# Two heads on the row halves of TensorE in a chunked gated linear attention

## Chip, cores and metric

The kernel runs on one core of one Trainium2 chip. The metric is the device time in microseconds of one execution. A core has five engines that the text names by the profile's short names: PE (TensorE: matmuls; PEld are its weight loads), DVE (VectorE), ACT (ScalarE), POOL (GpSimd) and SP (SyncE, which issues DMAs). Matmuls write into PSUM, which has 128 partitions and eight banks of 512 float32 per partition; the other operands lie in SBUF, also on 128 partitions. A matmul takes a stationary operand (rows by columns, loaded as weights) and a moving operand, and sums over the rows, which are the partitions of both. In the profile, `128*32 128x224` is a matmul of weights with 128 rows and 32 columns against 224 moving columns. A float32 matmul shows as two such records.

## The reference, cut to what matters

One layer of a streaming encoder: a normalised and modulated input is projected, two recurrences (GLA and HGRN2) of four heads each run over it, and their gated outputs are projected back. The prompt has 4096 positions, the sample 64. The recurrence is the same for both; GLA has 64 key features per head and HGRN2 has 128, both 128 value features:

```python
'''S_t = diag(exp g_t) S_{t-1} + k_t^T v_t,  o_t = q_t S_t.'''
def step(S, inp):                       # one chunk
    qc, kc, vc, gc = inp
    b = jnp.cumsum(gc, axis=2)
    o_inter = jnp.einsum('bhck,bhkv->bhcv', qc * jnp.exp(b), S)
    ...                                 # within the chunk: decayed q k^T, causal, times v
    S_new = (S * jnp.exp(b_last)[..., None]
             + jnp.einsum('bhck,bhcv->bhkv', kc * jnp.exp(b_last[:, :, None] - b), vc))
    return S_new, o_inter + o_intra.reshape(B, H, CHUNK, V)
```

All inputs and outputs are float32.

## The kernel before

The prompt is cut into 16 groups of 256 positions (two chunks of 128). First the GLA projections and recurrence run for all groups, then those of HGRN2, then the output projection. The sample's 64 positions lie beside the last GLA group and beside an early HGRN2 group.

`proj_gla` projects a group: queries and keys by feature (`proj_feat`, L559), the silu gate and the low-rank decay gate (`z_part`, L571 with 264 columns), values (L571 with 512 columns). These matmuls use float32 split into two parts, three products each. `x_turn` transposes the next group's input (L506) into the one bank `tp`, from which ACT (L515) and DVE (L517) take it.

`attend` is the recurrence over a group, as a generator that stops 14 times in GLA. Features lie on the partitions. GLA's heads have 64 features, so two heads share the 128 partitions: `NS` is 2, `G` (feature blocks per chunk) is 2 and `VG` (both chunks) is 4. HGRN2 has `NS` 1, `G` 4 and `VG` 8. The scores within a chunk are built by levels, blocks of positions that double:

- Positions 1, 2 and 4 apart: products by feature, turned by PE (L635) and summed by DVE (L641).
- `three_levels` does levels 2 to 4 at once. `prepare` fills a tile `wst` with queries decayed by distance (DVE L836, ACT L848, POOL memsets L846 and L843), PE multiplies them with blocks of 32 keys (L878) into a bank `at`, DVE picks the valid parts into `Ac` (`copy_predicated`, L892), ACT spreads these into the scores `A` (L898), and `times` (L836 on `Qg` and `K`) brings queries and keys to the next level.
- Levels 5 and 6, in a loop: matmuls into a bank `at` (L718), `step` on queries and keys (DVE L804 and L807), ACT copies into `A` (L728).
- Per chunk: keys by token (L740), outputs from the scores (L752) and from the state (L756) into the bank `o`, the state's increment (L764) into the bank `ms`, the new state (DVE L775), the gate's product (`done`, DVE L1082) and the squares for the norm (ACT L783), which read the bank `o`.

The array sums over all 128 rows, so in GLA the queries `Qg` are stored twice, once for each head of the pair, with the other head's 64 rows zero: ACT copies them there (L680). All work on `Qg` is then done per half, with DVE instructions on 64 partitions.

PSUM has three banks `pj` (projections), one `tp`, two `at`, one `o` and one `ms`, eight in all. A bank is handed on when all its readers are through.

The order of the work comes from `weave`: the projections of group g + 1 are the main generator (20 stops in GLA), and between its stops run the stops of `attend` of group g and of `x_turn`:

```python
sides = [(side, 12, 1, 18), (prep, 8, 0, 16)]
...
while s[4] * (last - first) < n * (m - first):
    s[4] += 1
    next(gen, None)
```

With 12 and 1 to 18, the steps 7 to 13 of `attend` come after the main stops 10, 11, 13, 14, 16, 17 and 19 (steps counted from the second stop of the generator on). A compiler pass then lays out each engine's queue; it keeps to this order by and large, and puts a later instruction first where it expects an earlier one to wait.

Of the kernel before, what the change touches and what calls it, by code (L numbers as in the profile page):

```python
# [10 lines left out]
AF = mybir.ActivationFunctionType  # L11
# [4 lines left out]
P = 128  # L16
# [5 lines left out]
# column offsets of w_in  # L22
# [6 lines left out]
class Kernel:  # L29
    def __init__(self, ctx, tc, t):  # L30
# [12 lines left out]
        # the second recurrence has the sample beside an earlier group  # L43
# [4 lines left out]
    # ---------------------------------------------------------------- helpers  # L48
# [53 lines left out]
    def wst(self):  # L102
        """Half of a staging tile; every second call takes a new one."""
# [8 lines left out]
    def split_w(self, st, tag, eng=None):  # L112
        """[H | L] of staged columns."""
# [5 lines left out]
    def weights(self, out, c, n, tag, stage=None, share=0):  # L119
        """Fills out with the units of columns c .. c + n, loads running ahead; a generator."""  # L120
# [11 lines left out]
    # ---------------------------------------------------------------- setup  # L132
    def setup(self):
# [66 lines left out]
    def ada_load(self, ap, k, few=()):  # L200
        """The columns of w_ada that shift and scale features k * 128 .. k * 128 + 128."""
# [11 lines left out]
    def first_group(self, ap, ada, w, rows):  # L213
        """Shift and scale of the conditioning, 128 features at a time, and with them the projections of
        group 0 that start the first recurrence: its sums run over the features as they come."""
# [46 lines left out]
        def modulate(k):  # L262
# [23 lines left out]
        # the array runs at its full rate only after some time of work  # L286
# [113 lines left out]
        # rank-16 gate: rows 0, 32, 64 hold hi, lo, hi of w_alpha  # L400
# [15 lines left out]
    def gate_rows(self):  # L416
        """gate * g_post for both conditionings, as rows in DRAM; a generator."""
# [27 lines left out]
        # the two parts of each product, and gate * g_post  # L445
# [16 lines left out]
    # ---------------------------------------------------------------- h = modulated norm of x, features on partitions  # L462
# [23 lines left out]
    def x_turn(self, g, raw=False):  # L486
        """hf = h of group g in float32, [128, 2, T] for two k each; a generator."""
# [43 lines left out]
    def split_h(self):  # L531
        """h in parts: of kt, [128, (hi, lo), T]."""
# [8 lines left out]
    def pair_up(self, h, rooms):  # L541
        """hi and lo of the sample side by side, as [128, 128] of kt."""
# [8 lines left out]
    def proj_feat(self, ps, W, c0, h, T):  # L551
        """[128 features, T]: the products of hi and lo parts that float32 keeps; a generator."""
# [22 lines left out]
    def pair_step(self, ps, both, r, wh, wl, kt):  # L575
        """both: hi and lo of r tokens side by side; rows r .. 2 r get what lo gives."""
# [4 lines left out]
    def fold(self, ps, r, n, tmp):  # L581
        """Adds rows r .. 2 r of n columns to rows 0 .. r."""
# [3 lines left out]
    def proj_tok(self, ps, W, c0, c1, h, o, r):  # L586
        """[r tokens, columns]; a generator with a stop half way."""
# [5 lines left out]
    # ---------------------------------------------------------------- chunks of a recurrence  # L593
    def attend(self, X, Q, K, F, rest, vs, S, CL, C, G, NS, done, table):
        """C chunks of CL tokens; a generator. X [128, 8, CL]: queries; K, F [128, C * G, CL]; vs[c]
        [CL, 512]. Heads lie on rows of 128 / NS features, NS of them in a group. S: the state before, in a list, which is replaced by the state after.
        done(c, o): called with the output of chunk c; returns where it is, and what to call with its
        reciprocal norms."""
# [19 lines left out]
        A = Af[:CL]  # L618

        # same position, and level 0: products by feature, turned and summed along features  # L620
# [29 lines left out]
        # level 0 of two heads side by side: of one by even positions, of the other by odd ones  # L650
# [19 lines left out]
        # level 1 by products too: a block of four has two keys by two queries  # L670
# [21 lines left out]
        T = self.step(K, Q, T, T_tile, 1, CL, C, G, NS)  # L692
# [782 lines left out]
```

## Time and profile before

| | us |
|---|---|
| median of 3 timed executions | 2234.81 (2232.6 to 2236.17) |
| profiled execution, first to last instruction | 2232.1 |
| GLA projections with the recurrence beside them, last increment of a group to that of the next | 49.35 to 49.43 in most groups |
| HGRN2, the same | 47.0 to 51.1 in most groups |
| output projection and what goes with it | the last 560 or so |

The page gives the execution's span, 2232.1; the time of the same execution with what lies around the span isn't given apart, so the timed median, 2.7 us above it, stands for it. In the rows below "busy" is the time in which an engine has something under way; a mean in ns is that of one instruction from its start to its end, and since several matmuls are under way at once, the time that one costs is read from the starts of neighbouring rows. An idle time in brackets stands with what ended it.

### The profile page before, as it was taken

How to read it: one execution, taken by the hardware profiler on the slowest of the kernel's cores; microseconds unless marked ns; L12 is line 12 of the kernel's file. 1: busy time of each engine (PE TensorE's matmuls, PEld its weight loads, DVE VectorE, ACT ScalarE, POOL GpSimd, SP SyncE). 2: the span in 40 equal slices, each digit the busy share in tenths (PEclk: the TensorE clock that was granted, in tenths of full speed). 3: DMA queues.
4: the chain of work that ended last, by engine and by line, in shares of the span. 5: the costliest groups of instructions: out<-in, count | busy, mean ns of one | idle time of the engine just before them, and what ended most of it. 6: DMA issues, size and time to landing. Idle time of an engine off the chain costs nothing.

```text
span 2232.1 us, 43696 instructions
## 1 busy us (share of the span) xinstructions
PE 2149.5 (96%) x15868; PEld 1878.6 (84%) x15868; DVE 1629.6 (73%) x5548; ACT 1014.9 (45%) x2822; POOL 264.9 (12%) x738
## 2 busy tenths in 40 slices
PE   7899999999999998999999999999989999999998
PEld 6788888888888887898989989999877888888887
DVE  6888788888877889868788788777795455444444
ACT  5656555555555565444444444444453222222212
POOL 3211111111111112111011000011041000000000
PEclk9999999999999999999999999999999999999999
DMA  9311111111111132111111111100235333333232
GB/s 259 114 56 69 48 53 51 51 51 55 64 61 48 54 103 64 50 46 43 56 45 48 44 34 55 48 30 30 68 123 162 120 101 132 128 118 123 100 108 91
DMA packets 98709, 173.11 MB, mean 78 GB/s; under 512 B 12669, under 2 KB 34657, under 8 KB 98493
## 3 DMA queue, kind: packets, MB, share of 16 engines
q1 hardware_dynamic: 98348, 170.05, 23.5%
q8 instruction: 125, 2.05, 0.4%
q14 instruction: 92, 0.75, 0.1%
q10 hardware_dynamic: 144, 0.26, 0.0%
HBM read 118.35 MB, written 51.93 MB: 76 GB/s over the span
## 4 chain that ended last, share of the span: by engine, by line
PE 66%; DVE 25%; ACT 4%; issue 2%; DMA 2%; SPq 0%; DVEq 0%; POOL 0%; ACTq 0%; POOLq 0%
PE ps_pj L1269 16%; PE ps_pj L571 15%; PE ps_pj L559 13%; DVE wst L836 8%; PE ps_at L571 6%; PE ps_o L752 2%; PE ps_o L756 2%; PE ps_at L878 2%; PE ps_ms L764 2%; PE ps_at L718 1%; DVE dd L641 1%; PE ps_at L635 1%; PE ps_tp L740 1%; DVE xt L484 1%; DVE Qg L807 1%
## 5 line engine op out<-in xcount | busy, mean ns | idle before, releaser
L571 PE MATMUL ps_pj<-wu,hh 128*128 128x512 f32 x1632 | 403.9, 397 | 2.5 <-DVE hh L91 1.4
L559 PE MATMUL ps_pj<-hh,wu 128*128 128x256 f32 (+1 forms) x2976 | 395.3, 287 | 0.0
L559 PEld LDWEIGHTS ps_pj<-hh,wu 128*128 128x128 f32 x2976 | 373.6, 191 | 4.7 <-issue 0.2
L571 PEld LDWEIGHTS ps_pj<-wu,hh 128*128 128x128 f32 x1632 | 297.6, 188 | 68.0 <-issue 6.2
L836 DVE TENSOR_TENSOR wst<-wst,T 64x80 f32<-64x80 f32 (+7 forms) x960 | 204.0, 226 | 15.4
L559 PE MATMUL ps_pj<-hh,wv 128*128 128x256 f32 (+1 forms) x1536 | 211.7, 289 | 0.0
L571 PE MATMUL ps_pj<-wv,hh 128*128 128x264 f32 x1464 | 204.5, 291 | 1.6 <-DVE wv L91 1.6
L559 PEld LDWEIGHTS ps_pj<-hh,wv 128*128 128x128 f32 x1536 | 191.5, 188 | 13.4 <-issue 11.1
L571 PEld LDWEIGHTS ps_pj<-wv,hh 128*128 128x128 f32 x1464 | 185.4, 189 | 9.9 <-issue 6.1
L1274 ACT ACTIVATE sq<-ps_pj 128x512 bf16<-128x512 f32 (+1 forms) x66 | 39.4, 597 | 297.0 <-PE ps_pj L1269 292.1
L90 ACT CAST hh<-hf 128x512 fp32r<-128x512 f32 (+1 forms) x188 | 117.5, 626 | 113.6 <-DVE hf L517 45.7
L1269 PE MATMUL ps_pj<-wv,ogh 128*128 128x512 f32 x512 | 162.6, 398 | 0.0
L1269 PE MATMUL ps_pj<-wu,ogh 128*128 128x512 f32 x512 | 158.4, 391 | 0.0
L571 PE MATMUL ps_at<-wu,hh 128*128 128x512 f32 x672 | 157.4, 390 | 0.0
L1135 ACT ACTIVATE g<-ps_pj 128x256 f32<-128x256 f32 (+1 forms) x128 | 49.5, 387 | 222.9 <-PE ps_pj L559 222.3
L571 PEld LDWEIGHTS ps_at<-wu,hh 128*128 128x128 f32 x672 | 126.0, 188 | 26.1
L91 DVE TENSOR_TENSOR hh<-hf,hh 128x512 fp32r<-128x512 f32 (+1 forms) x188 | 131.0, 700 | 22.3 <-ACT hh L90 20.6
L856 POOL COPY T<-T 128x16 f32<-128x16 f32 (+1 forms) x32 | 7.9, 246 | 932.4 <-DVE Qg L807 541.2
L1269 PEld LDWEIGHTS ps_pj<-wu,ogh 128*128 128x128 f32 x512 | 96.4, 188 | 20.9
L1269 PEld LDWEIGHTS ps_pj<-wv,ogh 128*128 128x128 f32 x512 | 94.2, 189 | 19.2
L1276 DVE TENSOR_TENSOR y_ss<-y_ss 128x1 f32<-128x1 f32 (+1 forms) x33 | 5.2, 159 | 136.4 <-ACT sq L1274 136.4
L1269 PE MATMUL ps_pj<-wv,ogl 128*128 128x512 f32 x256 | 101.2, 395 | 0.0
(294 smaller groups left out, 4029.8 us busy)
## 6 DMA issues: line engine op xcount, KB each, us to landing
xt<-in_x_prompt_dram SPq DMA_DIRECT2D x64, 512.0 KB
hf<-h_d SPq DMA_DIRECT2D x128, 256.0 KB
h_d<-hf SPq DMA_DIRECT2D x64, 256.0 KB
out_y_prompt_dram<-y SPq DMA_DIRECT2D x31, 512.0 KB
wst<-in_w_in_dram SPq DMA_DIRECT2D x36, 256.0 KB
ada_st<-in_w_ada_dram SPq DMA_DIRECT2D x32, 256.0 KB
oa_d<-e SPq DMA_DIRECT2D x32, 256.0 KB
oh_d<-e SPq DMA_DIRECT2D x32, 256.0 KB
```

The source lines that it names most:

```text
L90: self.nc.scalar.copy(hi, src)
L91: (eng or self.nc.vector).tensor_tensor(lo, src, hi.bitcast(F32), ALU.subtract)
L559: self.nc.tensor.matmul(ps[:, :T], a, b, start=i == 0, stop=i == n - 1)
L571: self.nc.tensor.matmul(ps[:r, : c1 - c0], a, b, start=kt == 0 and i == 0, stop=kt == KT - 1 and i == 2)
L752: nc.tensor.matmul(po[:, h, :], A[:, c * 4 + h, :], vs[c][:CL, h * P : (h + 1) * P], start=True, stop=St is None)
L756: nc.tensor.matmul(po[:, h, :], Q[:, h % NS, c * G + h // NS, :CL], St[:, h // NS, :], start=False, stop=True)
L764: nc.tensor.matmul(pd[s * w : (s + 1) * w, g, :], kc[:CL, g, s * w : (s + 1) * w], vs[c][:CL, h * P : (h + 1) * P], start=True, stop=True,)
L836: nc.vector.tensor_tensor(parts(dst), parts(src), t.unsqueeze(3).to_broadcast(shape), ALU.mult)
L878: nc.tensor.matmul(out, K[:, 2 // NS * pr + g, rows], rhs, start=True, stop=True)
L1135: nc.scalar.activation(sg, pf[:, :T], AF.Sigmoid)
L1269: nc.tensor.matmul(po[:r], a[:, kt, :r], b, start=m == 0, stop=m == 3 * KT - 1)
L1274: nc.scalar.activation(junk, po[:r], AF.Square, accum_out=ss[:, q : q + 1])
```

## The change

GLA's queries are no longer stored twice with zeros. `Qg` holds both heads of a pair on their own 64 rows, as the keys do, and each matmul that needs one head alone takes 64 rows of keys (or state) and 64 rows of queries. The two heads of a pair write into two different banks.

- `attend`: the queries go straight into `Qg`; the two ACT copies per group (L680) are gone. Levels 5 and 6 take two banks `at` and twice as many matmuls of half as many moving columns, and twice as many ACT copies of half the size. The outputs of even heads go into the bank `o`, those of odd heads into the upper half of the bank `ms`, whose lower half takes the state's increment. All four products with the scores come first, then the four with the state, in both recurrences.
- `three_levels`: pairs of feature blocks, not of heads; two calls of `prepare` per group instead of four, on 128 partitions; both banks `at` at once in GLA. DVE's picking of the scores (`place`) now comes before `times`, in both recurrences, and GLA has a stop between them. GLA's `attend` has 13 stops instead of 14.
- `step`: in GLA one instruction each for keys and queries instead of two and four. HGRN2's are the same as before.
- `done`: the gate's product in two parts where two banks hold the outputs.
- The sample (64 positions, both heads' scores in one bank) takes the odd heads' part from the state through a third place and adds it.

The weave's numbers are unchanged. The rest of the diff takes comments out.

```diff
@@ attend
-        q1 = Q[:, 0, :, :CL] if NS == 1 else q
+        q1 = Q
-        if NS == 2:
-            for s in range(2):
-                rr = slice(64 * s, 64 * s + 64)
-                nc.scalar.copy(Q[rr, s, :, :CL], q[rr])
...
-            pa = self.ps("at")[:CL, : NH * hf].rearrange("p (h j) -> p h j", h=NH)
+            pas = [self.ps("at")[:CL, : VG * hf].rearrange("p (g j) -> p g j", g=VG) for _ in range(NS)]
...
-                    nc.tensor.matmul(
-                        pa[r0 : r0 + m, g * NS : (g + 1) * NS, b * m : (b + 1) * m],
-                        K[:, g, s0 : s0 + m], Q2[:, :, g, b, :], start=True, stop=True,
-                    )
+                    for s, rr in enumerate(rows):
+                        nc.tensor.matmul(
+                            pas[s][r0 : r0 + m, g, b * m : (b + 1) * m],
+                            K[rr, g, s0 : s0 + m], Q2[rr, g, b, :], start=True, stop=True,
+                        )
...
             po = self.ps("o")[:CL].rearrange("p (h v) -> p h v", h=4)
+            pm = self.ps("ms")
+            pd = pm[:, : G * P].rearrange("p (g k) -> p g k", g=G)
+            pb = pm[:CL, G * P :].rearrange("p (g v) -> p g v", v=P)
+            apart = NS == 2 and CL == P
+            if apart:
+                pos = [po[:, :G], pb]
+                po = [pos[h % 2][:, h // 2, :] for h in range(4)]
...
             for h in range(4):
-                nc.tensor.matmul(
-                    po[:, h, :], A[:, c * 4 + h, :], vs[c][:CL, h * P : (h + 1) * P], start=True, stop=St is None
-                )
-                if St is not None:
+                v = vs[c][:CL, h * P : (h + 1) * P]
+                nc.tensor.matmul(po[h], A[:, c * 4 + h, :], v, start=h < n, stop=St is None and h == 4 - n)
+            if St is not None:
+                for h in range(4):
+                    s, g = h % NS, h // NS
+                    o = po[h] if apart or s == 0 else pb[:, g, :]
                     nc.tensor.matmul(
-                        po[:, h, :], Q[:, h % NS, c * G + h // NS, :CL], St[:, h // NS, :], start=False, stop=True
+                        o, Q[rows[s], c * G + g, :], St[rows[s], g, :],
...
@@ step
-        for c in range(C):
-            v = slice(c * G, c * G + G)
+        for o in range(0, VG, 4):
+            v = slice(o, min(o + 4, VG))
             nc.vector.tensor_tensor(K1[:, v], K1[:, v], Tsb[:, v], ALU.mult)
-            for s in range(NS):
-                rr = slice(64 * s, 64 * s + 64) if NS == 2 else slice(0, P)
-                nc.vector.tensor_tensor(Q2[rr, s, v], Q2[rr, s, v], Tfb[rr, v], ALU.mult)
+            nc.vector.tensor_tensor(Q2[:, v], Q2[:, v], Tfb[:, v], ALU.mult)
@@ three_levels
-        NP = C * G * NS // 2
+        VG = C * G
+        NP = VG // 2
...
-                pa = self.ps("at")
+                pas = [self.ps("at").rearrange("p (h c) -> p h c", h=4) for _ in range(NS)]
...
+                    for s, rr in enumerate(halves):
+                        nc.tensor.matmul(
+                            pas[s][rows, g0 + g], K[rr, 2 * pr + g, rows], Yt[rr, o : o + P], start=True, stop=True
+                        )
...
+                for s in range(NS):
+                    of = lambda a: a[:, hs].rearrange("p (g s) c -> p s g c", s=NS)[:, s]
+                    place(of(A), of(Ac), pas[s])
+                if NS == 2:
+                    yield
+                times(Q8[:, ns, 4:], Q8[:, ns, 4:], E8[:, ns, :7])
                 times(K8[:, ns, :28], K8[:, ns, :28], T8[:, ns, 1:])
@@ done, in attend_group
-                    nc.vector.tensor_tensor(ov, po, ov, ALU.mult)
+                    for b, pb in enumerate(pos):
+                        of = ov[:, b :: len(pos)]
+                        nc.vector.tensor_tensor(of, pb, of, ALU.mult)
```

More of the change, by code (lines that the diff above doesn't have):

```diff
@@ L618, in attend @@
         A = Af[:CL]
+        rows = [slice(0, P)] if NS == 1 else [slice(0, 64), slice(64, P)]
         def two(a):
@@ L705, in attend @@
         yield
-        T = yield from self.three_levels(A, Ac[:CL], Q[:, :, :, :CL], K, T, E, T_tile, CL, C, G, NS)
+        T = yield from self.three_levels(A, Ac[:CL], Q, K, T, E, T_tile, CL, C, G, NS)
         for l in range(5, L):
@@ L750, in attend @@
             po = self.ps("o")[:CL].rearrange("p (h v) -> p h v", h=4)
-            for h in range(4):
-                nc.tensor.matmul(
-                    po[:, h, :], A[:, c * 4 + h, :], vs[c][:CL, h * P : (h + 1) * P], start=True, stop=St is None
-                )
-                if St is not None:
+            pm = self.ps("ms")
[5 more added lines that the diff above has]
+                po = [pos[h % 2][:, h // 2, :] for h in range(4)]
+            else:
+                pos = [po]
+                po = [po[:, h, :] for h in range(4)]
+            n = NS if apart else 1
+            for h in range(4):
+                v = vs[c][:CL, h * P : (h + 1) * P]
[4 more added lines that the diff above has]
+                    o = po[h] if apart or s == 0 else pb[:, g, :]
                     nc.tensor.matmul(
-                        po[:, h, :], Q[:, h % NS, c * G + h // NS, :CL], St[:, h // NS, :], start=False, stop=True
-                    )
-            pd = self.ps("ms")[:, : G * P].rearrange("p (g k) -> p g k", g=G)
+                        o, Q[rows[s], c * G + g, :], St[rows[s], g, :],
+                        start=NS == 2 and not apart and h == 1,
+                        stop=h == 4 - NS or h == 3 and not apart,
+                    )
+                if NS == 2 and not apart:
+                    pd = self.ps("at")[:, : G * P].rearrange("p (g k) -> p g k", g=G)
+                    t = self.etile()[:CL, : G * P].rearrange("p (g v) -> p g v", v=P)
+                    nc.scalar.copy(t, pb)
+                    odd = pos[0][:, 1::2]
+                    nc.vector.tensor_tensor(odd, odd, t, ALU.add)
             for g in range(G):
@@ L765, in attend @@
                         pd[s * w : (s + 1) * w, g, :], kc[:CL, g, s * w : (s + 1) * w],
-                        vs[c][:CL, h * P : (h + 1) * P], start=True, stop=True,
+                        vs[c][:CL, h * P : (h + 1) * P], start=not apart, stop=not apart or g == G - 1,
                     )
@@ L787, in halved, with step @@
     @staticmethod
-    def halved(Q, m, CL):
-        return Q[:, :, :, :CL].rearrange("p s g (b two m) -> p s g b two m", two=2, m=m)
-    def step(self, K, Q, T, T_tile, l, CL, C, G, NS):
+    def halved(Q, m):
+        return Q.rearrange("p g (b two m) -> p g b two m", two=2, m=m)
+    def step(self, K, Q, T, T_tile, l, CL, VG):
         nc = self.nc
@@ L826, in three_levels @@
         T8, E8 = [x.rearrange("p g (b a) -> p (g b) a", a=8) for x in (T, E)]
[L827 to L831 removed]
+        K8, Q8 = [x.rearrange("p g (b r) -> p (g b) r", r=32) for x in (K, Q)]
+        halves = [slice(0, P)] if NS == 1 else [slice(0, 64), slice(64, P)]
+        n = 2 * B
         def times(dst, src, t):
@@ L840, in prepare, with place @@
             Yt = self.stage_pair() if B == 4 else self.wst()
-            Y = Yt[:, : 2 * B * STEP].rearrange("p (s n r) -> p s n r", s=NS, r=STEP)
-            if NS == 1:
-                nc.gpsimd.memset(Yt[:, 2 * B * STEP : 2 * B * STEP + 16], 0.0)
-            for s, rr in halves:
-                if NS == 2:
-                    nc.gpsimd.memset(Y[64 - 64 * s : 128 - 64 * s, s], 0.0)
-                q, y, t = Q8[s][:, ns], Y[rr, s], T8[rr, ns]
-                nc.scalar.copy(y[:, :, :28], q[:, :, 4:])
-                for a in range(2, 8):
-                    w = 4 * (8 - a)
-                    src = q[:, :, 8:] if a == 2 else y[:, :, off[a - 1] + 4 : off[a]]
-                    times(y[:, :, off[a] : off[a] + w], src, t[:, :, 1 : 9 - a])
-            return Yt
+            y, q, t = Yt[:, : n * STEP].rearrange("p (n r) -> p n r", r=STEP), Q8[:, ns], T8[:, ns]
+            nc.gpsimd.memset(Yt[:, n * STEP : n * STEP + 16], 0.0)
+            nc.scalar.copy(y[:, :, :28], q[:, :, 4:])
+            for a in range(2, 8):
+                w = 4 * (8 - a)
+                src = q[:, :, 8:] if a == 2 else y[:, :, off[a - 1] + 4 : off[a]]
+                times(y[:, :, off[a] : off[a] + w], src, t[:, :, 1 : 9 - a])
+            return Yt
+        def place(Ah, Ach, pa):
+            for a in range(1, 8):
+                w = 4 * (8 - a)
+                nc.vector.copy_predicated(
+                    Ach[:, :, 4 * a :].rearrange("p h (j m) -> p h j m", m=4),
+                    self.mask[:CL, : 8 - a].unsqueeze(1).unsqueeze(3).to_broadcast([CL, Ach.shape[1], 8 - a, 4]),
+                    pa[:CL, : Ach.shape[1], off[a] : off[a] + w].rearrange("p h (j m) -> p h j m", m=4),
+                )
+            for b in range(B):
+                nc.scalar.activation(
+                    Ah[:, :, 32 * b : 32 * b + 32], Ach, AF.Copy, scale=self.member[:CL, 8 + b : 9 + b]
+                )
         nc.gpsimd.tensor_copy(E8[:, :, 0], T8[:, :, 0])
@@ L860, in three_levels @@
         yield
-        ys.append(prepare(1))
+        if NP > 1:
+            ys.append(prepare(1))
         yield
@@ L879, in three_levels @@
             if pr + 2 < NP:
                 ys.append(prepare(pr + 2))
[L881 to L882 removed]
+            if pr % 2 or pr == NP - 1:
+                if pr < 2:
                     for i in range(6, 0, -1):
                         nc.gpsimd.tensor_tensor(T8[:, :, i], T8[:, :, i], T8[:, :, i + 1], ALU.mult)
[L885 to L902 removed]
```

88 lines of the change are left out of this document (29 added, 59 removed).

## Prediction

> **What bounds the kernel now.** I read the page's busy shares first, then the windows of the GLA stretch, of one of its groups and of the HGRN2 stretch, then the waits of PE, then PE's timeline over one group.
>
> ```profile
> PE 2149.5 (96%) x15868; PEld 1878.6 (84%) x15868; DVE 1629.6 (73%) x5548; ACT 1014.9 (45%) x2822; POOL 264.9 (12%) x738
> ```
>
> ```profile
> 137.00:876.00 739.00, 698.75 (x5572) 622.49 (x5572) 610.89 (x2368) 423.70 (x1288) 111.52 (x350) 1.00 0.18 59
> 435.76:485.12 49.36, 46.93 (x380) 41.95 (x378) 40.36 (x157) 28.12 (x88) 7.12 (x22) 1.00 0.15 54
> 1060.00:1676.00 616.00, 604.89 (x5429) 548.05 (x5428) 497.36 (x1613) 285.09 (x797) 86.98 (x245) 1.00 0.17 54
> ```
>
> ```profile
> PE ps_at L878 <- DVE wst L836: 17.9, 14, 1.9
> PE ps_tp L506 <- DVE hf L517: 15.8, 13, 1.2
> ```
>
> PE is busy for 96% of the span. The windows' rows give PE first, then PEld, DVE, ACT and POOL. In a GLA group of 49.36 us PE is busy for 46.93 and idle for 2.43, DVE is busy for 40.36, and the granted clock is 1.00. In HGRN2 PE is idle for 616 - 604.89 = 11.1 us in all. So GLA is bound by PE, plus 2.43 us of idle time per group that others cause. The waits say which: matmuls of `three_levels` (L878) wait for DVE's decayed queries (L836), 17.9 us in 14 groups, and the transposes L506 wait for DVE to empty their one bank (L517), 15.8 us in 13 groups. The timeline shows both places in one group:
>
> ```profile
> 451.60 0.66 PE L506 MATMUL ps_tp<-ident,xt 128*128 128x128 f32 x4 [1.21 <-DVE hf L517]
> ...
> 453.64 0.96 PE L878 MATMUL ps_at<-wst,K 128*32 128x224 f32 x16
> 454.54 1.73 PE L571 MATMUL ps_pj<-wv,hh 128*128 128x264 f32 x12
> ...
> 459.56 0.58 PE L878 MATMUL ps_at<-wst,K 128*32 128x224 f32 x8
> 461.37 0.59 PE L878 MATMUL ps_at<-wst,K 128*32 128x224 f32 x8 [1.22 <-DVE wst L836]
> 461.89 0.66 PE L506 MATMUL ps_tp<-ident,xt 128*128 128x128 f32 x4
> ```
>
> The two waits of 1.21 and 1.22 us are all of the group's idle time. DVE is 82% busy over the group, so it is behind in the stretch where these waits lie. The change therefore has two ways to save: less PE work for the attention, and less DVE work in front of PE. GLA's recurrences of groups 0 to 14 run beside the projections of groups 1 to 15, so what a group saves counts 15 times; the sixteenth runs beside HGRN2.
>
> **DVE, part by part.** The rows of one GLA group before:
>
> ```profile
> L836 DVE TENSOR_TENSOR wst<-wst,T 64x80 f32<-64x80 f32 (+4 forms) x40 | 8.2, 205 | 0.9
> ...
> L807 DVE TENSOR_TENSOR Qg<-Qg,T 64x128 f32<-64x128 f32 x12 | 3.3, 284 | 0.1
> L892 DVE COPY_PREDICATED Ac<-mask,ps_at 128x112 f32<-128x112 uint8 (+6 forms) x14 | 3.1, 220 | 0.1
> ...
> L836 DVE TENSOR_TENSOR wst<-Qg,T 64x96 f32<-64x96 f32 x8 | 2.0, 250 | 0.9 <-PE ps_at L878 0.8
> L804 DVE TENSOR_TENSOR K<-K,T 128x128 f32<-128x128 f32 x6 | 1.7, 284 | 0.1
> ...
> L836 DVE TENSOR_TENSOR Qg<-Qg,T 64x224 f32<-64x224 f32 x4 | 1.6, 393 | 0.1
> ...
> L1082 DVE TENSOR_TENSOR e<-ps_o,e 128x512 f32<-128x512 f32 x2 | 1.4, 688 | 1.1 <-PE ps_o L756 1.1
> ...
> L836 DVE TENSOR_TENSOR K<-K,T 128x224 f32<-128x224 f32 x2 | 0.8, 383 | 0.0
> ```
>
> In HGRN2 the same code already runs on 128 partitions. After the change GLA has half of its instructions (two calls of `prepare` against four):
>
> ```profile
> L836 DVE TENSOR_TENSOR wst<-wst,T 128x160 f32<-128x160 f32 (+4 forms) x20 | 4.6, 266 | 0.0
> ...
> L836 DVE TENSOR_TENSOR wst<-Qg,T 128x192 f32<-128x192 f32 x4 | 1.4, 345 | 0.0
> L836 DVE TENSOR_TENSOR Qg<-Qg,T 128x448 f32<-128x448 f32 x2 | 1.3, 641 | 0.0
> ...
> L836 DVE TENSOR_TENSOR K<-K,T 128x448 f32<-128x448 f32 x2 | 1.2, 621 | 0.1
> ```
>
> GLA's L836 comes to 8.2 + 2.0 + 1.6 + 0.8 = 12.6 us; half of HGRN2's 4.6 + 1.4 + 1.3 + 1.2 is 4.25. That saves 8.3. `step` is L807 and L804, 3.3 + 1.7 = 5.0 us in 18 instructions. After, it has six instructions on 128 partitions and up to 256 elements:
>
> ```profile
> L807 DVE TENSOR_TENSOR Qg<-Qg,T 128x256 f32<-128x256 f32 x96 | 42.2, 439 | 0.0
> ```
>
> Six at 0.44 are 2.6, which saves 2.4. The gate's product in two parts instead of one (L1082, 1.4 in a group) adds a start each; two of 256 elements at 0.44 against one at 0.69 is +0.2 per chunk, +0.4. L892 has the same 14 instructions. Sum: 10.3 us less per group, 40.36 down to about 30. By itself this is worth no more than the PE idle time that it ends.
>
> **ACT and POOL.** ACT loses the two copies into `Qg` and half of the copies in `prepare`, and gains six small copies per group in levels 5 and 6. At 424 us busy in 739 it isn't the bound, and I cost it at nothing; the cover is its own idle time, and where ACT stands in a chain it comes back in the bank rival below. POOL loses large memsets (111.5 us busy in 739, nothing waits for it on PE). No DMA moves and SP's queue is unchanged.
>
> **PE, part by part.** Levels 5 and 6 and a chunk's outputs, same group:
>
> ```profile
> 464.16 0.43 PE L718 MATMUL ps_at<-Qg,K 128*32 128x64 f32 x16
> 464.52 3.17 PE L571 MATMUL ps_pj<-wv,hh 128*128 128x264 f32 x24
> 467.62 0.66 PE L718 MATMUL ps_at<-Qg,K 128*64 128x128 f32 x8
> 468.21 3.02 PE L571 MATMUL ps_pj<-wu,hh 128*128 128x512 f32 x12
> ...
> 472.63 0.39 PE L752 MATMUL ps_o<-v,A 128*128 128x128 f32 x2
> 472.85 0.39 PE L756 MATMUL ps_o<-S,Qg 128*128 128x128 f32 x2
> 473.17 0.66 PE L764 MATMUL ps_ms<-v,kT 128*64 128x128 f32 x8
> 473.75 0.44 PE L740 MATMUL ps_tp<-ident,K 128*128 128x128 f32 x2
> ```
>
> From start to start a float32 matmul of 128 by 128 by 128 takes 472.85 - 472.63 = 0.22 us, so 0.11 per record. Column tiles run side by side: L764's eight records on 64 columns take 473.75 - 473.17 = 0.58, four pairs at 0.11 and 0.14 more; entering that form costs 473.17 - 472.85 - 0.22 = 0.10. HGRN2 shows 32 columns:
>
> ```profile
> 1271.33 0.64 PE L878 MATMUL ps_at<-wst,K 128*32 128x128 f32 x16
> 1271.90 2.75 PE L559 MATMUL ps_pj<-hh,wv 128*128 128x256 f32 x21
> 1274.58 0.46 PE L718 MATMUL ps_at<-Qg,K 128*32 128x32 f32 x32
> 1274.97 1.45 PE L559 MATMUL ps_pj<-hh,wv 128*128 128x256 f32 x10
> ```
>
> Sixteen records in 0.57 us are four sets of four at 0.11 and 0.13 for the change of form. No row before shows two row halves side by side, so that is the unknown. I take it that they overlap as the column tiles do, since that is the nearest row; the other end is no overlap.
>
> - L878 before: 0.90 (453.64 to 454.54) + 0.58 + 0.52 = 2.00 us for 32 records of 224 columns. After: 64 records of 128 columns, in eights 8 sets at 0.11. In two bursts 0.89 + 0.26 = 1.15, in one 1.02. Without overlap 16 sets and 0.13 are 1.91. Taken: -0.85; bounds -0.98 and -0.09.
> - Level 5 before: 0.36. After: 32 records of 32 columns; HGRN2 has 32 of them in 0.39. Taken +0.03; bounds 0 and +0.03.
> - Level 6 before: 0.59. After: 16 records of 64 columns, which overlapped take half of the 0.44 plus 0.15, 0.37; without overlap 0.59. Taken -0.19; bounds -0.22 and 0.
> - Outputs from the state: eight records per chunk, 0.89. After, as pairs, what L764 takes with its entry, 0.58 + 0.10, less a part of the change that L764 pays already: 0.65. Twice -0.24, so -0.48. Bounds: -0.62 (0.58 each) and +0.48 (no overlap and two changes of form).
> - The four products with the scores first: the same instructions, 0.
>
> Sum of PE's work: -1.5 us per group, bounds -1.8 and +0.4.
>
> A row against a rule: 32 records of L718 in 0.39 us are 12 ns each. The Trainium skill, page "TensorE: Matmul & The Clock Gate", section "Part 1: The HAM clock gate", says that starts of matmuls are never closer than about 25 ns however few columns they have. This speaks against cutting matmuls in two. By that figure, an estimate, L878's 64 records would need 1.6 us and level 5's 32 would need 0.8, and the sum of PE's work would be -0.6 instead of -1.5, the time about 2201. The trace does not agree for column tiles.
>
> The stalls: with DVE 10 us lighter, and the whole of `prepare` two calls ahead of L878, the wait for L836 has no cause left, and L517 isn't queued behind as many small products. What is late next is the chain through the two `at` banks (below). I take -1.7 of 2.43, leaving 0.7 us; bounds -2.43 and +1.5.
>
> **Other places.** The 16th GLA recurrence saves its PE work only, 1.5 us. HGRN2's `place` before `times` puts seven `copy_predicated` of 0.22 ahead of the products that level 5 needs; PE there has projection matmuls to put in front (the row at 1271.90 runs straight after L878), so 0.1 per group, 2 us in all, and nothing where this cover holds. The sample's extra copy and add: under 1 us, once.
>
> **Sum.** Per group -1.5 - 1.7 = -3.2; times 15 is -48; with -1.5 + 2 + 1 it is -46.5. From the profiled 2232.1 this gives 2185.6. The median of the timed runs lies 2.7 above, so 2188.
>
> **The rivals.**
>
> *Halves don't overlap, stalls go.* PE's work at its upper bound: +0.4 - 1.7 = -1.3 per group, -20: 2215. For it: no row of 64 rows. Against it: the column tiles overlap fully. The Trainium skill, page "TensorE: Matmul & The Clock Gate", section "Part 3: Packing small matmuls", says that row tiles run at once and gives 3.07 for four of them; no run here shows it.
>
> *The stalls stay.* If L506's wait comes from the single bank `tp` and not from DVE's load, and another wait takes L878's place one for one, only PE's -1.5 is left: -22, 2212. For it: only one `tp` bank exists. Against it: the releaser is a DVE instruction in a stretch where DVE is full.
>
> *The two `at` banks chain.* Each level now takes both, so L718 of level 5 waits for both halves of `place`, and level 6 for level 5's copies. Behind L718 on PE stand the gate's projections, and behind those DVE's and ACT's work on them.
>
> ```profile
> 418.41 1.26 ACT L898 ACTIVATE A<-Ac,member 128x128 f32<-128x128 f32 x4
> 419.58 1.04 ACT L728 COPY A<-ps_at 32x128 f32<-32x128 f32 x4
> ```
>
> ```profile
> L783 ACT ACTIVATE sq<-ps_o 128x128 bf16<-128x128 f32 x128 | 35.5, 278 | 13.1 <-DVE e L1082 10.6
> ```
>
> After L878 DVE has 14 x 0.22 + 0.6 = 3.7 us of its own plus the gate path's products; PE has three stops of 12 records up to level 5, some 4.7 us. That about fits, up to 1 us late. Level 6 is one stop (1.6 us and the transposes) after level 5, and before it ACT has the second half of L898 (1.26) and eight L728 at 0.26 (2.1): 1.4 or more late. The second chunk now follows the first by one stop of about 3 us, in which ACT's four squares (at least 4 x 0.28) and DVE's products must free `o` and `ms`: up to 0.5. Together about 2.9 to 3.9 us against 2.43 now. With PE's -1.5 the kernel ends between 2221 and 2236; the middle, about 2229, taken. Against it: the compiler pass puts other matmuls in front where it sees the wait.
>
> *A change of row half costs like a change of form* (the other side). The entry into another form costs 0.10 in the rows above. If each alternation of the halves costs that, 32 + 16 + 8 + 8 matmuls per group alternate 64 times: +6.4 - 1.7 = +4.7 per group, +70: 2305. It turns the result slower from 1.7 / 64 = 0.03 us per alternation on. Against it: L764 alternates its column halves at no such cost.
>
> *A floor per small record.* Level 5 before has 0.36 / 16 = 22 ns per record. If this is a floor for rows in halves, L878 takes 1.44, level 5 0.72 and level 6 0.36; PE's work is -0.9: 2199. The Trainium skill's floor, told above, is of the same kind.
>
> *Better than taken:* all idle time gone and one burst, -1.8 - 2.43 = -4.2 per group: 2171.
>
> **Numbers.** Chances: forecast 0.42 (own range 2176 to 2204); floor 0.08; no overlap 0.11; stalls stay 0.11; bank chain 0.16; alternation 0.06; better 0.06. The likeliest gives 2188. From 2168, just beyond the better case, to 2226, a third into the bank chain, 0.83 are held. A measurement of this kernel tells 0.2%, 4.5 us, from no change. Faster: all but the alternation and half of the bank chain, 0.86; same 0.05 and slower 0.09, from the bank chain's other half (0.05 and 0.03) and the alternation (0.06).
>
> **What would show it.** Right: L836 in a GLA group near 4.3 us, DVE near 30; L878 in eights with starts close together and 0.11 per set; the products with the state in pairs, 0.6 to 0.7 per chunk; no wait of L878 for L836; a group period near 46.1. Wrong: L718 or the second chunk's outputs waiting for L892, L728 or L783 (bank chain); records of the two halves following each other at 0.11 (no overlap) or more (alternation); L506 still waiting for L517. The prediction fails most likely if the two `at` banks cost PE more than 1 us per group.

## The result and the profile after

The changed kernel takes 2171.31 us (median of four executions, 2167.58 to 2171.88) against 2233.93 (2232.6 to 2236.17) for the kernel before on the same chip: a ratio of 0.9718, with a 95% interval of 0.9704 to 0.9731. That is 62.6 us less, where 46.5 had been predicted. Ratios and ranges here leave out a few executions that were disturbed, at other granted clocks than their neighbours or several times as long.

The profiles are of single executions; the changed kernel's is that of 2167.58 us.

Lines have moved: L836 of before is L861 after, L804 and L807 are L830 and L831, L878 is L908, L892 is L879, L752, L756 and L764 are L770, L775 and L791, L740 and L742 are L745 and L747, L1082 is L1102. First the page's busy shares, then one steady GLA group (the windows view, columns PE, PEld, DVE, ACT, POOL, clock):

```profile
PE 2121.3 (98%) x16776; PEld 1868.9 (86%) x16776; DVE 1448.8 (67%) x4735; ACT 979.4 (45%) x2790; POOL 237.1 (11%) x636
```

```profile
437.90:482.73 44.83, 44.83 (x436) 41.21 (x438) 29.78 (x107) 25.88 (x84) 4.79 (x16) 1.00 0.17 60
```

The group went from 49.36 to 44.83 us. PE's idle time of 2.43 us is gone altogether (44.83 busy of 44.83), and its busy time fell from 46.93 by 2.1. DVE went from 40.36 to 29.78. The waits of the GLA stretch (138 to 700 us; us in total, times, longest) show neither L861 nor L517 any more:

```profile
PEld ps_ms L791 <- ACT kT L747: 5.4, 9, 1.7
...
PE ps_ms L791 <- ACT kT L747: 3.8, 4, 1.5
PEld ps_at L718 <- ACT A L728: 2.5, 13, 0.2
```

What PE still waits for lies in four groups only and is ACT's. The wait through the two `at` banks is the last line, 0.2 us at a time on the weight loads. Past 700 us, where the sample's work comes in, it shows twice on PE itself: L718 waits for ACT's L728 for 1.77 us at 748.03 and for 0.94 us at 805.16. DVE's groups in the same GLA group:

```profile
L861 DVE TENSOR_TENSOR wst<-wst,T 128x160 f32<-128x160 f32 (+4 forms) x10 | 2.2, 266 | 0.0
...
L830 DVE TENSOR_TENSOR K<-K,T 128x256 f32<-128x256 f32 x3 | 1.3, 419 | 1.6 <-PE ps_at L718 1.6
L831 DVE TENSOR_TENSOR Qg<-Qg,T 128x256 f32<-128x256 f32 x3 | 1.3, 417 | 0.0
...
L861 DVE TENSOR_TENSOR wst<-Qg,T 128x192 f32<-128x192 f32 x2 | 0.7, 348 | 0.0
L861 DVE TENSOR_TENSOR Qg<-Qg,T 128x448 f32<-128x448 f32 x1 | 0.6, 625 | 0.0
L861 DVE TENSOR_TENSOR K<-K,T 128x448 f32<-128x448 f32 x1 | 0.6, 618 | 0.0
```

L861 comes to 2.2 + 0.7 + 0.6 + 0.6 = 4.1 us (12.6 before), the two lines of `step` to 2.6. PE's timeline in that group, with the row behind a burst where its cost is read from the starts:

```profile
463.40 1.16 PE L908 MATMUL ps_at<-wst,K 64*32 64x128 f32 x64
464.49 0.75 PE L571 MATMUL ps_pj<-wv,hh 128*128 128x264 f32 x4
...
469.52 0.35 PE L718 MATMUL ps_at<-Qg,K 64*32 64x32 f32 x32
469.81 0.66 PE L506 MATMUL ps_tp<-ident,xt 128*128 128x128 f32 x4
...
472.08 0.46 PE L718 MATMUL ps_at<-Qg,K 64*64 64x64 f32 x16
472.47 0.76 PE L571 MATMUL ps_pj<-wv,hh 128*128 128x264 f32 x4
...
475.71 0.39 PE L770 MATMUL ps_o<-v,A 128*128 128x128 f32 x2
...
476.91 0.27 PE L775 MATMUL ps_o<-S,Qg 64*128 64x128 f32 x1
476.92 0.27 PE L775 MATMUL ps_ms<-S,Qg 64*128 64x128 f32 x1
477.02 0.27 PE L775 MATMUL ps_o<-S,Qg 64*128 64x128 f32 x1
477.03 0.27 PE L775 MATMUL ps_ms<-S,Qg 64*128 64x128 f32 x1
...
477.37 0.66 PE L791 MATMUL ps_ms<-v,kT 128*64 128x128 f32 x8
```

L775 shows the row halves best: a record for the even head and one for the odd head start within 0.01 us of each other, and the next pair starts 0.11 us later, the time that one record alone cost before. The 64 records of the three levels (64 rows, 128 moving columns) take 464.49 - 463.40 = 1.09 us where 32 of 128 rows and 224 columns took 2.00.

From the first query projection of GLA (L559) to the first of HGRN2 the time fell from 773.8 to 709.2 us, 64.6. HGRN2, from its first query projection to its last, took 752.9 and takes 752.8.

### The profile page after: what moved, and what is told of

Same layout as the page of the kernel before. It is cut to its first block, busy times and chain, and to the rows that moved or that the text cites. A ratio compares the mean times of both kernels' runs of the same rounds, so it can differ in the third digit from the quotient of the medians.

```text
span 2165.8 us, 44469 instructions
## 1 busy us (share of the span) xinstructions
PE 2121.3 (98%) x16776; PEld 1868.9 (86%) x16776; DVE 1448.8 (67%) x4735; ACT 979.4 (45%) x2790; POOL 237.1 (11%) x636
## 4 chain that ended last, share of the span: by engine, by line
PE 86%; DVE 7%; ACT 3%; DMA 3%; issue 1%; POOL 0%; SPq 0%; DVEq 0%; ACTq 0%; POOLq 0%
PE ps_pj L571 22%; PE ps_pj L559 22%; PE ps_pj L1287 16%; PE ps_at L571 7%; PE ps_at L908 2%; PE ps_ms L791 2%; PE ps_at L638 2%; PE ps_o L775 2%; PE ps_o L770 2%; DMA xt<-in_x_prompt_dram 2%; DVE wst L861 1%; PE ps_tp L506 1%; PE ps_at L718 1%; PE ps_tp L745 1%; PE ps_pj L579 1%
## 5 line engine op out<-in xcount | busy, mean ns | idle before, releaser
L571 PE MATMUL ps_pj<-wu,hh 128*128 128x512 f32 x1632 | 405.3, 397 | 3.3 <-DVE hh L91 2.4
L559 PE MATMUL ps_pj<-hh,wu 128*128 128x256 f32 (+1 forms) x2976 | 395.6, 287 | 0.0
L559 PEld LDWEIGHTS ps_pj<-hh,wu 128*128 128x128 f32 x2976 | 373.8, 191 | 4.6 <-issue 0.3
L571 PEld LDWEIGHTS ps_pj<-wu,hh 128*128 128x128 f32 x1632 | 297.6, 188 | 65.5 <-issue 3.5
L559 PE MATMUL ps_pj<-hh,wv 128*128 128x256 f32 (+1 forms) x1536 | 214.1, 289 | 0.0
L559 PEld LDWEIGHTS ps_pj<-hh,wv 128*128 128x128 f32 x1536 | 192.5, 188 | 14.9 <-issue 12.9
L571 PE MATMUL ps_pj<-wv,hh 128*128 128x264 f32 x1464 | 203.2, 290 | 1.6 <-DVE wv L91 1.6
L571 PEld LDWEIGHTS ps_pj<-wv,hh 128*128 128x128 f32 x1464 | 184.5, 188 | 6.5 <-issue 3.1
L571 PE MATMUL ps_at<-wu,hh 128*128 128x512 f32 x672 | 158.5, 392 | 0.0
L571 PEld LDWEIGHTS ps_at<-wu,hh 128*128 128x128 f32 x672 | 126.9, 189 | 26.4
L861 DVE TENSOR_TENSOR wst<-wst,T 128x160 f32<-128x160 f32 (+4 forms) x480 | 118.1, 263 | 4.0
L1287 PE MATMUL ps_pj<-wu,ogl 128*128 128x512 f32 x256 | 99.7, 390 | 0.0
```

Of the source, the lines that this page charges most:

```text
L559: self.nc.tensor.matmul(ps[:, :T], a, b, start=i == 0, stop=i == n - 1)
L571: self.nc.tensor.matmul(ps[:r, : c1 - c0], a, b, start=kt == 0 and i == 0, stop=kt == KT - 1 and i == 2)
L861: nc.vector.tensor_tensor(parts(dst), parts(src), t.unsqueeze(3).to_broadcast(shape), ALU.mult)
L1287: nc.tensor.matmul(po[:r], a[:, kt, :r], b, start=m == 0, stop=m == 3 * KT - 1)
```

## Experiments

Theory: PE works less because the halves run at once, and its waits go because DVE has fewer instructions. Rivals: DVE's part alone, or the smaller number of bursts and stops, gives the gain.

### DVE's work undone alone, the order of the halves, and both

First, DVE's instructions cut back to 64 partitions (`step` and the `times` of K and Q likewise):

```diff
-                times(y[:, :, off[a] : off[a] + w], src, t[:, :, 1 : 9 - a])
+            for ms in [slice(i * k, i * k + k) for i in range(NS)]:
+                for rr in halves:
...
+                        times(y[rr, ms, off[a] : off[a] + w], src, t[rr, ms, 1 : 9 - a])
```

> The changed kernel with DVE's GLA instructions of prepare (products), times and step cut again into the instructions of the kernel before: 64 rows at a time, and by half the blocks. PE's matmuls stay those of the changed kernel. Theory (DVE's load made the two waits): DVE in a GLA group goes from 30 back to about 40 us, waits of L908 for L861 or of L506 for L517 come back, +1.5 to +2.4 us per group, 15 groups: 2194 to 2207 us. Rival (the waits went because all of the three levels' matmuls now come in one burst with both calls of prepare issued two stops ahead, or because of the order of the queues): DVE's load is hidden, within 5 us of 2171.

Measured: 2288.8 to 2302.4 us, ratio 1.0285 (1.0256 to 1.0314). DVE's instructions are as many and as small as before, and the kernel is not merely as slow as before but some 64 us slower, beyond both expectations.

Second, all of one half's matmuls of a burst ahead of the other's:

```diff
-            for g in range(2):
-                for b in range(B):
+            for s, rr in enumerate(halves):
+                for g, b in [(g, b) for g in range(2) for b in range(B)]:
...
-                for h in range(4):
+                for h in (0, 2, 1, 3) if apart else range(4):
```

> The changed kernel with the same matmuls in another order: all of the even heads' first, then all of the odd heads', in the three levels, in levels 5 and 6, and heads 0, 2, 1, 3 in the products with the state. So two matmuls that follow each other hardly ever lie on different row halves. Theory (overlap of the row halves is what PE saves): three levels 16 sets at 0.11 instead of 8, +0.8; products with the state +0.44 per chunk, +0.88; level 6 +0.2, level 5 up to +0.1: +1.9 us per group, 15 groups: about 2200 us (2192 to 2205). Rival (PE saves because of fewer columns and fewer bursts, the halves overlap little): at most +0.5 per group, below 2179 us.

Measured: 2171.3 to 2173.0 us, ratio 0.973 (0.9713 to 0.9746), the same as the changed kernel. That is where the rival had been put, that the halves overlap little. The timeline of this kernel:

```profile
464.30 1.38 PE L908 MATMUL ps_at<-wst,K 64*32 64x128 f32 x64
465.61 0.63 PE L571 MATMUL ps_pj<-wv,hh 128*128 128x264 f32 x3
```

The burst takes 1.31 us instead of 1.09, far from the 1.95 that it takes without halves (below). The rows of L908 don't tell which half a record is of. Those of L775 do, by their banks: a record of an even head and one of an odd head still start 0.01 to 0.02 us apart (477.86 `ps_o` and 477.87 `ps_ms`, then 478.07 and 478.09), though the kernel writes both even heads first. So the halves still run at once here, and the rival doesn't follow from the time. Whether PE starts one half's records while the other's wait, or the compiler's layout mixed them again, stays open. What is shown is that the order in which the kernel writes the halves hardly matters, and that this run is no test of the overlap.

Both together:

> Both of these together: DVE's instructions cut again, and the halves one after the other. Left of the change: no zeros, no ACT copies into Qg, no large POOL memsets, one burst for the three levels, one stop less. Theory (PE's work and DVE's load add up and are all of the change): the sum of the two losses, about 2230 us, that is within 8 us of before. Rival (the losses hide each other, PE being slower leaves DVE time): clearly less than the sum, 2200 to 2215 us.

Measured: 2302.23 us (2295.12 to 2304.31), ratio 1.0316 (1.0299 to 1.0333), far above both expectations. This one's profile stands for the first experiment too (waits from 138 to 800 us, then windows inside one group):

```profile
PE ps_at L914 <- DVE wst L864: 31.3, 20, 1.7
PE ps_tp L506 <- DVE hf L517: 26.7, 13, 2.1
```

```profile
363.00:366.00 3.00, 2.90 (x25) 2.69 (x23) 2.82 (x14) 0.56 (x1) 0.00 (x0) 1.00 0.00 0
366.00:369.00 3.00, 0.99 (x9) 1.00 (x10) 2.73 (x13) 1.02 (x3) 0.00 (x0) 1.00 0.07 27
...
372.00:375.00 3.00, 0.84 (x24) 0.38 (x24) 2.83 (x12) 0.00 (x0) 1.53 (x6) 0.84 0.23 87
375.00:378.00 3.00, 3.00 (x21) 2.81 (x14) 3.00 (x19) 0.00 (x0) 0.11 (x1) 0.50 0.01 3
```

Two things happen. All 48 small products of `prepare` now stand ahead of one burst, and DVE runs without a pause (2.7 to 3.0 of each 3 us) while PE waits up to 2.1 us for them. And after such waits the granted clock falls, here to 0.50, so that PE's own work takes longer too. The waits of before, 1.2 us each, cost no clock.

### The same small products in two lots

```diff
-        if NP > 1:
+        if NP > 1 and NS == 1:
             ys.append(prepare(1))
...
+            if NS == 2 and pr + 1 < NP:
+                ys.append(prepare(pr + 1))
+                yield
+                yield
```

> The first experiment again (VectorE's products on 64 partitions at a time, twice as many), but the 48 small products of a group stand in two lots of 24 with stops and a burst of matmuls between them, as the kernel before had them. If the first one's 2300 us came from 48 products ahead of one burst (stalls of 1.7 to 2.1 us, after which the granted clock fell to 0.57 to 0.72), the stalls shrink to those of before (2.4 us a group) and the clock stays at 1.00: 2171 + 15 x 2.4 + some 5 for a second burst = 2212 us (2195 to 2240). If VectorE's load alone makes the stalls, it stays near 2300 (2270 or more).

Measured: 2248.66 us (2245.55 to 2249.6), ratio 1.0061 (1.0047 to 1.0074). Spreading the products takes back about 48 of the 125 us by which the first experiment lies above the changed kernel. Both expectations missed: the placement was a large part of it, not all. One group, and the waits from 138 to 700 us:

```profile
445.20:495.17 49.97, 46.05 (x437) 41.36 (x436) 39.94 (x159) 25.95 (x84) 4.05 (x17) 1.00 0.16 54
```

```profile
PE ps_tp L506 <- DVE hf L517: 35.2, 22, 2.3
```

This is the kernel that has PE's part of the change and DVE's instructions of before. PE's busy time is 0.9 us below that of before (46.05 against 46.93), DVE's is 39.94 against 40.36, and the period is 49.97 against 49.36: what PE saves comes back as waiting for DVE. With DVE near 40 us of a group, the faster PE gains nothing in this placement. The stops are not those of before, and L506 waits up to 2.3 us here where it waited 1.2, so how much of the waiting is due to the placement that is left isn't separated.

### Less work for DVE in the kernel before

The kernel before, where `prepare` only clears the second head's tile and skips its products and its copy; this part of the scores is left out.

```diff
                 q, y, t = Q8[s][:, ns], Y[rr, s], T8[rr, ns]
+                if s == 1:
+                    nc.gpsimd.memset(y, 0.0)
+                    continue
```

> The kernel before, in which prepare leaves out DVE's products and ACT's copy for the second head of each pair; POOL clears those rows instead. The scores between parts of a block are then left out for odd heads. PE's instructions stay the same. DVE loses about 5 us per GLA group. Theory (DVE's load makes the waits): PE's 2.4 us idle per group go, 15 groups: 2198 us (2195 to 2208). Rival (the one bank tp and the order of the queues make the waits): 2225 us or more.

Measured: 2188.45 us (2186.74 to 2191.13), ratio 0.9805 (0.979 to 0.9819), better than expected. PE's 15868 instructions are those of before. A group:

```profile
424.60:471.12 46.52, 46.52 (x381) 42.04 (x379) 34.84 (x133) 27.06 (x82) 9.05 (x26) 1.00 0.17 58
```

With DVE at 34.84 us PE never waits: 49.36 falls to 46.52, by the idle 2.43 and 0.41 of PE's own. So DVE's part alone (with 1.1 us less on ACT, whose copies went with it) is worth 2.84 us of the 4.53, and 5.5 us less on DVE is enough for that. Whether the shorter group of the changed kernel needs all of its 10.6 wasn't tried.

### No row halves, all else as changed

Each matmul on a half takes all 128 rows, so that the two heads of a pair are summed into both results.

```diff
-                            K[rr, g, s0 : s0 + m], Q2[rr, g, b, :], start=True, stop=True,
+                            K[:, g, s0 : s0 + m], Q2[:, g, b, :], start=True, stop=True,
...
-                            pas[s][rows, g0 + g], K[rr, 2 * pr + g, rows], Yt[rr, o : o + P], start=True, stop=True
+                            pas[s][rows, g0 + g], K[:, 2 * pr + g, rows], Yt[:, o : o + P], start=True, stop=True
...
-                        o, Q[rows[s], c * G + g, :], St[rows[s], g, :],
+                        o, Q[:, c * G + g, :], St[:, g, :],
```

> The changed kernel, with each matmul that used half of the rows now using all 128: the two heads of a pair are summed into both results, so the scores and outputs are other numbers, but the count of records, their columns, the banks and all of VectorE's work stay. This takes the row halves away from TensorE alone. By my theory TensorE, busy all the time in GLA, gets back the time that it spent before: 0.9 us a group in the three levels, 0.3 in levels 5 and 6, 0.4 in the outputs, 1.7 in all (46.52 us of the light kernel against 44.85), so 2171 + 15 x 1.7 = 2196 us (2188 to 2202). If the gain came from VectorE and from fewer bursts, and not from the halves at once, 2171 to 2175.

Measured: 2189.96 us (2188.26 to 2191.86), ratio 0.9801 (0.9787 to 0.9814). It falls in the expected range, 19 us above the changed kernel (the spans of the two profiled executions differ by 24.3). A group, and the timeline of the same bursts:

```profile
424.50:471.13 46.63, 46.63 (x436) 43.26 (x435) 30.01 (x107) 26.03 (x84) 4.80 (x17) 1.00 0.16 58
```

```profile
429.88 2.02 PE L908 MATMUL ps_at<-wst,K 128*32 128x128 f32 x64
431.83 0.39 PE L571 MATMUL ps_pj<-wv,hh 128*128 128x264 f32 x1
...
436.88 0.49 PE L718 MATMUL ps_at<-Qg,K 128*32 128x32 f32 x32
437.30 0.66 PE L506 MATMUL ps_tp<-ident,xt 128*128 128x128 f32 x4
...
439.57 0.73 PE L718 MATMUL ps_at<-Qg,K 128*64 128x64 f32 x16
440.23 0.51 PE L571 MATMUL ps_pj<-wv,hh 128*128 128x264 f32 x2
```

Same records, columns, banks and DVE work; PE is busy all the time in both. The halves alone are worth 46.63 - 44.83 = 1.80 us a group: in the three levels 1.95 against 1.09, in level 5 0.42 against 0.29, in level 6 0.66 against 0.39, and in the outputs of a chunk 1.88 (443.47 to 445.35) against 1.66, twice.

### Bursts, HGRN2's order, and the last wait

A stop between the two lots of 32 records in GLA:

```diff
+            if NS == 2 and pr == 0 and NP == 2:
+                yield
```

> The changed kernel with one stop more in GLA: the 64 records of the three-level products are sent as two bursts of 32 with other work of TensorE between them. The records stay the same. If fewer bursts are a part of what the change gave (an entry costs 0.1 us, and the neighbours on both sides lose their overlap), a group grows by 0.2 to 0.4 us, and the time by 15 times that: 2175 us (2173 to 2178). If bursts cost nothing, 2171.

Measured: 2167.41 us (2166.53 to 2169.25), ratio 0.9701 (0.9687 to 0.9714): no slower.

```profile
458.90:504.13 45.23, 45.23 (x437) 41.17 (x436) 30.33 (x107) 25.87 (x84) 4.80 (x17) 1.00 0.18 60
```

The second burst does cost 45.23 - 44.83 = 0.40 us in a steady group, as expected. But all groups take 45.2 here, whereas the changed kernel's take 44.83 to 46.41, 45.18 in the mean, since L791's waits for `kT` are gone in this one. One cancels the other. That fewer bursts gave the gain is ruled out as its main cause.

HGRN2 with `times` ahead of `place`, as before:

```diff
+                def on():
+                    times(Q8[:, ns, 4:], Q8[:, ns, 4:], E8[:, ns, :7])
+                    times(K8[:, ns, :28], K8[:, ns, :28], T8[:, ns, 1:])
+
+                if NS == 1:
+                    on()
                 for s in range(NS):
...
                 if NS == 2:
                     yield
-                times(Q8[:, ns, 4:], Q8[:, ns, 4:], E8[:, ns, :7])
-                times(K8[:, ns, :28], K8[:, ns, :28], T8[:, ns, 1:])
+                    on()
```

> The changed kernel, with the order of before put back in HGRN2 alone: the products of Q and K with the decays (times) ahead of the copies into the scores (place). If the order is what lengthened HGRN2's steady groups from 47.03 to 47.47 us and from 48.4 to 48.8, both go back: 14 or 15 groups x 0.44 = 6 us, so 2165 us (2162 to 2168), and level 5 is one burst of 32 records again. If the two banks or the longer list of records does it, the time stays at 2171 (2169 to 2173). GLA is the same in both.

Measured: 2167.6 us (2163.11 to 2169.49), ratio 0.9692 (0.9679 to 0.9706), which lies in the range expected if the order matters. But its span of 2167.7 is not below the changed kernel's 2165.8, HGRN2 takes 752.6 us against 752.8, and its steady groups are 47.47 to 47.59 as in the changed kernel. So the order is not what lengthened them; the few us between the medians have no place in the two profiles, and the intervals of the two ratios touch (up to 0.9706 here, from 0.9704 there). The timelines of a steady HGRN2 group, before and then changed, show what differs in a group that is 0.44 us longer:

```profile
1411.28 1.08 PE L878 MATMUL ps_at<-wst,K 128*32 128x128 f32 x32
1414.65 0.65 PE L878 MATMUL ps_at<-wst,K 128*32 128x128 f32 x16 [0.20 <-DVE wst L836]
1415.54 0.64 PE L878 MATMUL ps_at<-wst,K 128*32 128x128 f32 x16
```

```profile
1436.16 0.65 PE L908 MATMUL ps_at<-wst,K 128*32 128x128 f32 x16
1439.39 0.65 PE L908 MATMUL ps_at<-wst,K 128*32 128x128 f32 x16
1442.52 0.64 PE L908 MATMUL ps_at<-wst,K 128*32 128x128 f32 x16
1445.96 0.65 PE L908 MATMUL ps_at<-wst,K 128*32 128x128 f32 x16
1447.10 0.33 PE L718 MATMUL ps_at<-Qg,K 128*32 128x32 f32 x16 [0.18 <-DVE K L861]
1448.27 0.33 PE L718 MATMUL ps_at<-Qg,K 128*32 128x32 f32 x16
```

Three bursts of the three levels became four, spread over 10 us instead of 4; level 5's one became two, and level 6's two became one. Why the compiler lays them out so, with HGRN2's code nearly unchanged, stays open.

Last, the wait that is left in GLA. ACT's timeline in the changed kernel, where PE waited 1.49 us at 252.56:

```profile
250.69 1.06 ACT L479 ACTIVATE hf<-xt 128x1024 bf16<-128x1024 f32 x1 [1.09 <-DMA xt<-in_x_prompt_dram]
...
251.86 0.39 ACT L1005 ACTIVATE e<-ps_pj 128x264 f32<-128x264 f32 x1
252.15 0.37 ACT L747 COPY kT<-ps_tp 128x256 f32<-128x256 f32 x1
```

The copy of `kT` stands behind the squares of the next input, which wait for their DMA. Moving the copy to DVE:

```diff
-            nc.scalar.copy(kT[:CL], pk)
+            (nc.vector.tensor_copy if apart else nc.scalar.copy)(kT[:CL], pk)
```

> The changed kernel, with the copy of the turned keys (kT) in GLA on VectorE instead of ScalarE. In the changed kernel TensorE's only waits left in GLA are the state's increments that wait for this copy (5.4 us over 13 groups, up to 1.5 us at once), where ScalarE stands behind the squares of the next input (1.06 us) that wait for their DMA. VectorE has 15 us of room in a group of 45. If that is all of it, the period is 44.84 us in every group and the time falls by 13 to 15 times 0.34, to 2166 us (2164 to 2169). If VectorE's queue is as late at that place, it stays at 2171 or rises (2171 to 2180).

Measured: 2169.87 to 2174.08 us, ratio 0.9728 (0.9714 to 0.9742): nothing gained. The waits from 138 to 704 us:

```profile
PEld ps_o L771 <- ACT sq L811: 6.4, 12, 1.9
...
PE ps_o L771 <- ACT sq L811: 3.0, 3, 1.5
```

The wait for `kT` is gone, and in the same three groups PE now waits for the norm's squares (L811), which come late on ACT after the same instruction and hold the bank `o`. The cause is ACT behind the input's DMA, not the copy. No version was found that beats the changed kernel by more than can be measured.

## Why the prediction was right, and where its sizes were off

- *Two ways to save, PE's work and DVE in front of PE*: right, and the runs separate them. From 49.36 the lighter DVE leads to 46.52, and the row halves from 46.63 to 44.83.
- *The stalls, -1.7 of 2.43*: the largest mis-sized term. All 2.43 went, and the kernel before with DVE lightened, which doesn't wait either, shows that 0.41 of PE's busy time goes with them: 2.84 us in place of 1.7. The 0.7 us left for "what is late next" was put on the `at` banks; what came is ACT's `kT`, 0.34 us in the mean (45.18 - 44.84).
- *PE's work, -1.5*: measured -2.1, of which the 0.41 went with the waits; 1.69 is left for the change of PE's work itself (46.52 to 44.83), a little more than was taken. Its parts were right where they could be seen: L878 -0.85 predicted, 2.00 to 1.09 measured; level 6 -0.19, 0.59 to 0.39; outputs -0.48, two times 0.22. Level 5 was put at +0.03 and came out at -0.07. The rest, about 0.5, lies in rows that the prediction didn't price; 0.2 of it is in the gate's projections around the bursts (L571 with 264 columns, 12.57 to 12.37 us from start to start), and more than half of that went with the waits, since the lightened kernel has 12.44 there.
- *DVE 10.3 us less*: 40.36 to 29.78, 10.6. The gate's product cost +0.3 (1.38 to 1.68) instead of +0.4.
- *Row halves overlap as column tiles do*: right, 1.95 against 1.09 for the same 64 records. The rivals of no overlap and of dear alternation fall with that.
- *A floor per small record*: fell. 32 records of level 5 take 0.29 us, 9 ns each. The Trainium skill's floor of about 25 ns between starts (page "TensorE: Matmul & The Clock Gate", section "Part 1: The HAM clock gate") would make that 0.8 us; the trace doesn't agree for records on separate row and column tiles.
- *The `at` banks chain*: 0.2 us at a time on PEld in the steady groups, where PE has projections to put in front at each of these places: it is busy for all of the 44.83 us. Where the sample's work comes in the chain does show: L718 waits 1.77 and 0.94 us for L728, once each.
- *Stalls stay, for want of a second `tp` bank*: fell. The changed and the lightened kernel still have one bank `tp`, and L506 waits for L517 in neither; with DVE at 39.94 us it waits 35.2 us in all. So the load on DVE makes this wait.
- *The case called better than taken* (2171) named the time that came; its -4.2 us a group stands against 4.25. The time lies outside the forecast's own range (2176 to 2204) and inside the whole one (2168 to 2226) through this case, which was given 0.06: the forecast was right on what saves, and both its terms were too small.
- *The sixteenth recurrence -1.5, HGRN2 +2, the sample +1*: HGRN2's steady groups cost +0.44, not +0.1, and not because of `place`. The first group of HGRN2, beside which the sixteenth GLA recurrence and the sample's run, gave it back: 55.88 to 49.07 us, 6.8 less. The prediction let that recurrence save PE's work only; PE's idle time in this group fell by 2.4 us as well, and its busy time by 4.4. The three terms were put at +1.5 together and came out near 0 (752.9 to 752.8), by luck.

The sum: 15 groups at 49.43 - 45.18 = 4.25 are 64, against the 48 of the prediction; the rest of the kernel hardly moved.

## What to carry to other kernels

When PE is busy for 95% and waits for 5%, ask first what the engine behind the waits has left: here PE's saving of 1.8 us a group counts in full with DVE at 30 of 45 us and comes to nothing with DVE at 40 of 50. A layout that uses full partitions on DVE and row halves on PE saves on both. The two parts don't depend on each other alike: the lighter DVE alone took the kernel before from 2233 to 2188 us, while PE's part showed as a gain only where DVE was light. When a wait is moved to another engine, look at what stands ahead of the waiting instruction in its queue before moving the instruction itself.

## What the runs showed of the hardware

- Two float32 matmuls on different row halves and into different banks start within 0.01 us of each other and run together. A burst of 64 goes in 1.09 us, as against 1.95 on full rows.
- Waits of PE can cost twice. In the kernel with both parts undone, after waits of 2.0 to 2.1 us, with another of 1.5 to 1.7 some us later, the granted clock fell to 0.50 for some us; after the 1.2 us of before it stayed at 1.00. The length alone doesn't decide: in the kernel with two lots PE waits 2.2 to 2.3 us once in each of 13 groups between 138 and 800 us, yet the clock fell in five only. What decides there is where the wait lies. The clock changes only at points that are multiples of 3.41 us apart. In the five groups at least 2.17 us of idle time fall between two such points, and the next 3.41 us run at 0.50; in the other eight a point cuts the wait, at most 1.89 us lie on one side, and the clock stays. One of each (3.41 us before and after a point; the last column but two is the clock):

```profile
248.60:252.01 3.41, 1.16 (x11) 0.95 (x10) 3.12 (x16) 0.68 (x2) 0.00 (x0) 1.00 0.00 0
252.01:255.43 3.42, 3.42 (x45) 2.80 (x43) 3.09 (x16) 1.49 (x4) 0.00 (x0) 0.50 0.25 84
...
296.40:299.81 3.41, 2.52 (x21) 2.31 (x20) 3.16 (x17) 0.60 (x2) 0.64 (x3) 1.00 0.00 0
299.81:303.22 3.41, 2.04 (x16) 1.90 (x16) 3.10 (x15) 1.19 (x2) 0.00 (x0) 1.00 0.21 77
```

This is no threshold for other kernels: with both parts undone, stretches with 1.6 to 1.85 us of idle time are followed by 0.50 in some groups and by 1.00 in others, and what else counts there stays open.

The Trainium skill, page "TensorE: Matmul & The Clock Gate", section "Part 1: The HAM clock gate", has the clock halve after an idle window of about 3.4 us that runs freely. The spacing of 3.41 us, and that a wait's place against it decides, agree with a freely running window. PE was never idle for more than 2.3 us at a time here, so a window that is idle throughout is not what these traces show.
